# First conditioning weights, norm and first V, q, k products taken in two halves of the features; rope tables on two engines

## The chip, the cores and the metric

The kernel runs on one core of a Trainium2 chip. The metric is the device time of one execution in microseconds (us), shown as the median of several runs. One further execution was recorded by the hardware profiler; every row below comes from it. Engines are named as the profile names them: PE is TensorE (PEld its weight loads), DVE is VectorE, ACT is ScalarE, POOL is GpSimd, SP is the queue that issues the DMAs.

## The reference

Two transformer blocks over 512 tokens of 1024 features. Only the opening of the first block is touched by the change:

```python
def first_block(x, c, positions, ada_w, ada_b, norm_mix_g, ...):
    cond = jax.nn.silu(c)
    for layer in range(DEPTH):
        mod = (cond @ ada_w[layer] + ada_b[layer])[:, None, :]
        shift_m, scale_m, gate_m, shift_f, scale_f, gate_f = jnp.split(mod, 6, axis=-1)
        h = rmsnorm(x, norm_mix_g[layer]) * (1.0 + scale_m) + shift_m
        ...
            mixed = attention_head_groups(h, positions, attn_w_in[i], attn_w_out[i])
```

`attention_head_groups` multiplies `h` by `attn_w_in` to get q, k and V; q and k of the first group of heads are turned by `partial_rope` with the cosine and sine of position times frequency.

## The kernel before

Everything is in float32, feature by token: `x` is eight tiles of 128 features x 512 tokens (k = 0..7). To keep precision each factor of a product is split into a high and a low part (`hh`, `hl` of `h`; `whi`, `wlo` of the weights), and `mm3` (L243, L244, L245) adds three products for each k. The order of the instructions on each engine is set before the run by a scheduler that lists them by data and program order; each engine then works through its own list in that order and stops where an operand is missing.

The opening of `block1` does this. The queue SP loads constants, `x`, the positions (`pi`) and then 32 tiles `araw` of the conditioning weights, 128x512 each, twelve buffers deep. Each `araw` is multiplied by the vector `cond`: for half of the four column groups on PE (L306, one output row), for the others on DVE (L309 and L311, into `acc`). L328 turns each sum of 512 into four columns of `mod` (four matmuls with a vector of ones), and L330 adds the bias. Groups 2 and 3 of 512 columns make the scale (all of A, L336, before the shift's weights come), groups 0 and 1 the shift B. Beside it `mean_squares` (L377, L378, L383), `rstd` (on POOL, `rs_r`) and `bcast_rows` (L367, into PSUM) make the reciprocal root of the norm. `modulated` then makes `t2u` = x A r (L396, DVE), `hh` = `t2u` + B (L397, ACT) and `hl` (L398, DVE), and only with that can the first products start: V of the first four heads (96 matmuls of 256 columns), then q and k of the first two heads (24 matmuls of 512 columns each).

After it, `project` turns q and k by the rope tables (L669 to L673), splits them and copies them by DMA into `stk`, `stk2h` and `stk2l` (L684), the operands of the first scores `sc` (L729). The products q and k of the next two heads are in PE's list between the first k and the first scores, and so fill PE while the rope chain runs.

`rope_tables` makes both tables on POOL, one after the other with the same scratch tiles. Its instructions stand in POOL's list before and after `rs_r`.

Of the kernel before, what the change touches and what calls it, by code (L numbers as in the profile page):

```python
# [9 lines left out]
F32 = mybir.dt.float32  # L10
# [129 lines left out]
class Net:  # L140
# [95 lines left out]
            steps.append(step)  # L236
        return steps

    def mm3(self, out, terms):

        n = len(terms)
        for j, (lh, ll, rh, rl) in enumerate(terms):
            self.nc.tensor.matmul(out, lhsT=lh, rhs=rh, start=j == 0, stop=False)  # L243
            self.nc.tensor.matmul(out, lhsT=ll, rhs=rh, start=False, stop=False)  # L244
            self.nc.tensor.matmul(out, lhsT=lh, rhs=rl, start=False, stop=j == n - 1)  # L245

    def mm_fm(self, out, w, c0, h, kt=KD, m=P):

# [342 lines left out]
        if cols:  # L591
            nc.vector.tensor_mul(dst, u, ps[0:64, n:2 * n])

    def v_heads(self, pool, w, c0, h, n, tag, bufs=1):


        V = pool.tile([P, n // P, 4, 2, 64], F32R, tag=tag, bufs=bufs, name="V")
        for t in range(0, n // P, 2):
            ps = self.psum()
            for i in range(2):  # L600
                self.mm_tm(ps[:, i * 256:i * 256 + 256], w, c0, 256, h, t + i)
            src = ps.rearrange("p (t h d) -> p t h d", t=2, h=4)
            self.split(V[:, t:t + 2, :, 0], V[:, t:t + 2, :, 1], src)
        return V

    def rope_tables(self, pool, work):

        nc = self.nc
        eng = nc.gpsimd
        pi = work.tile([P, T], I32, name="pi")  # L610
        nc.sync.dma_start(pi, self.a["pos"].to_broadcast([P, T]))
        ang, k, t, r = [work.tile([P, T], F32, name="rp_" + n) for n in ("ang", "k", "t", "r")]
        eng.tensor_copy(ang, pi)
        eng.tensor_scalar(ang, ang, self.c_inv, None, op0=ALU.mult)

        c1 = 6.28125
        c2 = math.floor((TWO_PI - c1) * 2 ** 20) / 2.0 ** 20
        c3 = TWO_PI - c1 - c2
        magic = 1.5 * 2.0 ** 23
        lim = 3.1415925  # L620
        out = []
        for name, turn in (("cos", 0.25), ("sin", 0.0)):
            eng.tensor_scalar(k, ang, 1.0 / TWO_PI, turn, op0=ALU.mult, op1=ALU.add)
            eng.tensor_scalar(k, k, magic, None, op0=ALU.add)
            eng.tensor_scalar(k, k, magic, None, op0=ALU.subtract)
            for c, y in ((c1, ang), (c2, r), (c3, r)):
                eng.tensor_scalar(t, k, c, None, op0=ALU.mult)
                eng.tensor_sub(r, y, t)
            if turn:
                eng.tensor_scalar(r, r, math.pi / 2, None, op0=ALU.add)  # L630
            o = pool.tile([P, T], F32, name="rp_" + name)
            eng.tensor_scalar(o, r, lim, -lim, op0=ALU.min, op1=ALU.max)
            out.append(o)

        def finish():
            for o in out:
                self.tc.keep_in_program_order(nc.scalar.activation(o, o, AF.Sin))
            eng.tensor_scalar(out[1], out[1], self.c_sgn, None, op0=ALU.mult)
            return out
        return finish  # L640

    def attention(self, x, h, gate, w_in, w_out, norms):
        nc = self.nc
        swap = [(j + 8 if j < 8 else j - 8) if j < 16 else j for j in range(32)]
        with self.pool("early", side="right") as ep, self.pool("att") as ap:
            self.work = self.letters(ep, b=2) | self.letters(ap, d=2) | dict(big=(ap, "stk1", 2))
            self.exp_and_ln(h[1][:, KD - 1])
            cos, sin = self.rope_cs
# [4 lines left out]
            def project(c, m, V):  # L653

                part, base = c // 2, c // 2 * 1536
                c0 = base + c % 2 * 256
                if m == 0:
                    w = self.wchunk(w_in[:, c0 + 1024:c0 + 1280], "k")
                    V = self.v_heads(ap, w, 0, h, T, "V", 2)
                    self.w_qk = [self.wchunk(w_in[:, c0 + j * 512:c0 + j * 512 + 256]) for j in range(2)]  # L660
                st = []
                for j in range(2):
                    ps = self.psum()
                    self.mm_fm(ps, self.w_qk[j], m * P, h)
                    scale = 0.125 if j == 0 else 1.0
                    hl = [ap.tile([P, T], F32R, tag="s" + x, bufs=2, name="s" + x) for x in "hl"]
                    if part == 0:
# [1149 lines left out]
    def block1(self, x):  # L1817
# [7 lines left out]
        b = self.v("ada_b", 0, 48)  # L1825
        with self.pool("rope", side="right") as rp:
            with self.dense():
                for k in range(0, KD, 4):
                    nc.sync.dma_start(x[:, k:k + 4], a["xT"][k * P:(k + 4) * P].rearrange("(k p) t -> p k t", p=P))
                self.c_inv = self.load_const(rp, "inv")  # L1830
                self.c_sgn = self.load_const(rp, "sgn")
                with self.pool("acc", side="right") as self.accp:
                    rope = self.rope_tables(rp, self.accp)
                    self.causal = self.load_const(rp, "causal", BF16)
                    self.lt01 = self.load_const(rp, "lt01")
                    self.ltneg = self.load_const(rp, "ltneg", BF16)
                    self.negtri = self.load_const(rp, "negtri", F32R)
                    self.work["u"] = (self.accp, 8, "t2u", T)
                    tasks = self.ada_tasks(a["ada_w"][0], (1, 0), [cond], [mod], b, 12, "dn", (1, 3), False)
                    A = fx.tile([P, KD], F32, tag="A1", bufs=3, name="A")  # L1840
                    h, ((stats, apply),) = self.hnorm(x, T, A, mod[:, 0:8], size=T)
                    w = a["attn_w_in"][0][:, 1024:1280]
                    loads = self.load_ahead(*[(w, 0, k, "k") for k in (0, 4)])
                    for i in range(32):
                        tasks[i // 16 * 16 + (1 - i % 2) * 8 + i % 16 // 2]()
                        if i == 7:
                            stats()
                        if i == 15:
                            self.gain_scale(A, self.v("norm_mix_g", 0, 8), mod, 1)
                    for load in loads:  # L1850
                        load()
                    apply()
# [11 lines left out]
            self.attention(x, h, mod[:, 16:24], a["attn_w_in"][0], a["attn_w_out"][0],  # L1864
                           lambda: norms("norm_ffn_g", 0, 3, *self.ffn_first(*self.gate_up(a["ffn_w_in"][0]))))
# [69 lines left out]
```

## Time and profile before

| what | value |
| --- | --- |
| median of 3 runs | 3423.15 us (3422.83 to 3424.58) |
| profiled execution, its time | 3421.65 us |
| its span | 3419.9 us |
| mean granted clock of PE, of full speed | 0.981 |
| PE busy | 3247.7 us (95%) |
| DVE busy | 2228.5 us (65%) |
| ACT busy | 1275.0 us (37%) |
| POOL busy | 100.0 us (3%) |

The span is the recorded part of the execution; the profiled execution took 1.75 us more than its span and 1.5 us less than the median of the runs. Busy is the share of the span in which an engine had an instruction in work. All times in the rows count from the start of the span.

### The profile page before, as it was taken

To read this page: it belongs to the slowest core of one execution; us is meant where nothing else is said; L and a number is where in the kernel's file an instruction comes from. 1 tells how busy PE (TensorE), PEld (TensorE's weight loads), DVE (VectorE), ACT (ScalarE), POOL (GpSimd) and SP (SyncE) were. 2 spreads that over 40 slices of the span, in tenths; PEclk is the share of its full clock that TensorE was granted. 3 is DMA by queue.
4 is the path that set the end of the run, shared out by engine and by line. 5 is a ranking of instruction groups with operands and counts; after the bars stand their busy time and mean duration, and the time that the engine had idled before them with its cause. 6 is when DMAs were issued, how large, how long until landed. Compare 5 with 4: busy or idle time off the path is not lost.

```text
span 3419.9 us, 46640 instructions
## 1 busy us (share of the span) xinstructions
PE 3247.7 (95%) x17648; PEld 2666.4 (78%) x17648; DVE 2228.5 (65%) x4569; ACT 1275.0 (37%) x2467; POOL 100.0 (3%) x142
## 2 busy tenths in 40 slices
PE   7998999999999899998999989999999889889999
PEld 4886788878778787887777768888887776778886
DVE  6977655568988677677878777534445875753334
ACT  3566422235443332223644443212123455542222
POOL 4000000001000000000000000000000000000000
PEclk9999999999999999999999999999999999999999
DMA  6645355532111254553343323333332443413332
GB/s 226 173 134 163 119 168 157 158 114 62 44 50 56 64 172 138 163 167 108 115 133 89 113 62 98 113 95 111 117 111 75 114 133 102 127 50 96 96 97 76
DMA packets 480081, 389.76 MB, mean 114 GB/s; under 512 B 21360, under 2 KB 390128, under 8 KB 479856
## 3 DMA queue, kind: packets, MB, share of 16 engines
q1 hardware_dynamic: 479856, 386.77, 37.9%
q8 instruction: 139, 2.28, 0.3%
q14 instruction: 86, 0.70, 0.1%
HBM read 356.28 MB, written 17.83 MB: 109 GB/s over the span
## 4 chain that ended last, share of the span: by engine, by line
PE 43%; DVE 4%; ACT 3%; issue 1%; DMA 1%; POOL 0%; POOLq 0%; DVEq 0%; ACTq 0%
PE dn L243 6%; PE dn L244 6%; PE dn L245 6%; PE d L243 6%; PE d L245 6%; PE d L244 6%; PE s L1244 1%; PE tp L1208 1%; PE tp L1227 1%; PE tp L1234 1%; DVE cv L1373 1%; ACT pr L1187 1%; DVE wlo L173 1%; PE dn L378 1%; DVE st L1184 0%
## 5 line engine op out<-in xcount | busy, mean ns | idle before, releaser
L172 ACT CAST whi<-raw 128x1024 fp32r<-128x1024 f32 (+1 forms) x399 | 417.1, 1046 | 782.7 <-PE d L245 411.3
L173 DVE TENSOR_TENSOR wlo<-raw,whi 128x1024 fp32r<-128x1024 f32 (+1 forms) x399 | 486.3, 1220 | 268.5 <-ACT whi L172 267.8
L243 PE MATMUL dn<-hh,whi 128*128 128x512 f32 (+1 forms) x1688 | 619.7, 368 | 8.9 <-ACT t2b L1358 4.5
L245 PE MATMUL dn<-hl,whi 128*128 128x512 f32 (+1 forms) x1688 | 614.0, 365 | 0.0
L244 PE MATMUL dn<-hh,wlo 128*128 128x512 f32 (+1 forms) x1688 | 613.3, 364 | 0.0
L243 PE MATMUL d<-hh,whi 128*128 128x512 f32 (+1 forms) x1120 | 400.7, 358 | 0.0
L244 PE MATMUL d<-hh,wlo 128*128 128x512 f32 (+1 forms) x1120 | 399.9, 357 | 0.0
L245 PE MATMUL d<-hl,whi 128*128 128x512 f32 (+1 forms) x1120 | 399.8, 357 | 0.0
L243 PEld LDWEIGHTS dn<-hh,whi 128*128 128x128 f32 x1688 | 321.4, 191 | 57.8 <-ACT t2b L1358 5.2
L245 PEld LDWEIGHTS dn<-hl,whi 128*128 128x128 f32 x1688 | 321.1, 191 | 46.5 <-issue 2.7
L244 PEld LDWEIGHTS dn<-hh,wlo 128*128 128x128 f32 x1688 | 321.7, 191 | 42.7 <-issue 1.4
L311 DVE SCALAR_TENSOR_TENSOR acc<-araw,cond,acc 128x512 f32<-128x512 f32 x322 | 241.9, 751 | 68.3 <-DMA araw<-in_ada_w 38.7
L243 PE MATMUL d<-gh,whi 128*128 128x512 f32 (+1 forms) x696 | 252.3, 363 | 0.4 <-ACT gh L172 0.4
L244 PE MATMUL d<-gh,wlo 128*128 128x512 f32 (+1 forms) x696 | 249.8, 359 | 0.0
L245 PE MATMUL d<-gl,whi 128*128 128x512 f32 (+1 forms) x696 | 248.6, 359 | 0.0
L243 PEld LDWEIGHTS d<-hh,whi 128*128 128x128 f32 x1120 | 210.7, 188 | 32.6 <-issue 1.3
L244 PEld LDWEIGHTS d<-hh,wlo 128*128 128x128 f32 x1120 | 210.7, 188 | 32.5 <-issue 1.3
L245 PEld LDWEIGHTS d<-hl,whi 128*128 128x128 f32 x1120 | 210.7, 188 | 31.6 <-DVE hl L398 0.9
L243 PEld LDWEIGHTS d<-gh,whi 128*128 128x128 f32 x696 | 130.6, 188 | 27.9 <-issue 3.5
L245 PEld LDWEIGHTS d<-gl,whi 128*128 128x128 f32 x696 | 130.1, 188 | 24.5 <-issue 2.2
L244 PEld LDWEIGHTS d<-gh,wlo 128*128 128x128 f32 x696 | 130.6, 188 | 23.5 <-issue 2.2
L515 DVE TENSOR_TENSOR t2b<-t2a,d 128x512 f32<-128x512 f32 (+1 forms) x67 | 42.0, 627 | 150.7 <-PE d L245 150.7
(507 smaller groups left out, 5641.9 us busy)
## 6 DMA issues: line engine op xcount, KB each, us to landing
araw<-in_ada_w SPq DMA_DIRECT2D x192, 256.0 KB, 3.7
araw<-in_w_ada SPq DMA_DIRECT2D x192, 256.0 KB, 3.0
raw<-in_ffn_w_in SPq DMA_DIRECT2D x88, 512.0 KB, 4.2
raw<-in_ffn_w_out SPq DMA_DIRECT2D x44, 512.0 KB, 4.4
raw<-in_w_in SPq DMA_DIRECT2D x44, 512.0 KB, 3.8
raw<-in_w_gate SPq DMA_DIRECT2D x44, 512.0 KB, 3.9
raw<-in_w_up SPq DMA_DIRECT2D x44, 512.0 KB, 3.8
raw<-in_w_down SPq DMA_DIRECT2D x44, 512.0 KB, 3.6
```

The costliest lines, as they stand in the source:

```text
L172: nc.scalar.copy(hi, src)
L173: nc.vector.tensor_sub(lo, src, hi.bitcast(F32))
L243: self.nc.tensor.matmul(out, lhsT=lh, rhs=rh, start=j == 0, stop=False)
L244: self.nc.tensor.matmul(out, lhsT=ll, rhs=rh, start=False, stop=False)
L245: self.nc.tensor.matmul(out, lhsT=lh, rhs=rl, start=False, stop=j == n - 1)
L311: nc.vector.scalar_tensor_tensor(st[i], raw, s, st[i], op0=ALU.mult, op1=ALU.add)
L378: nc.tensor.matmul(sums, lhsT=weights(k), rhs=sq, start=k == 0, stop=k == KD - 1)
L515: nc.vector.tensor_mul(y, s, pu[:, :n])
L1187: nc.scalar.activation(pr, s, AF.Exp, bias=st[:, 0:1], accum_out=st[:, 2:3])
L1208: nc.tensor.transpose(tp[:, n * P:(n + 1) * P], pr[:, c:c + P], self.ident)
L1227: nc.tensor.matmul(ps[:64, q0:q1], lhsT=lhs, rhs=pt[sl // 2][0][:, sl % 2, q0:q1].bitcast(F32), start=j == 0, stop=j == nb - 1, skip_group ...
L1234: nc.tensor.matmul(ps[:, q0:q1], lhsT=lhs, rhs=pt[sl // 2][i][:, sl % 2, q0:q1], start=j == 0 and i == 0, stop=j == nb - 1 and i == 1, ski ...
```

## The change

The 32 tasks of the conditioning weights are taken in another order: first the tiles of scale and shift for features 0 to 511, then those for features 512 to 1023. After each half A and B of these features are known, `hh` and `hl` of its four k are made, and the products of V, q and k are added up over these four k only. Four PSUM banks (two `tp` for q and k, two `dn` for V) hold the sums from the first half to the second. The norm is no longer folded into `t2u`: `xr` = x r is made once for all eight k on DVE as soon as the broadcast r stands in PSUM; then `hh` = A xr + B on ACT and `t2u`, `hl` on DVE. The conditioning work on PE is now the shift (groups 0 and 1), that on DVE the scale. The first weights of V, q and k are loaded between the conditioning weights.

The sine table moves from POOL to DVE, with scratch tiles of its own, and the first two steps of the angle too; the positions are loaded before `x` and no longer after it.

```diff
+    def mm3(self, out, terms, start=True, stop=True, **kw):
...
-        eng = nc.gpsimd
...
-        eng.tensor_copy(ang, pi)
-        eng.tensor_scalar(ang, ang, self.c_inv, None, op0=ALU.mult)
+        nc.vector.tensor_copy(ang, pi)
+        nc.vector.tensor_scalar(ang, ang, self.c_inv, None, op0=ALU.mult)
...
-        for name, turn in (("cos", 0.25), ("sin", 0.0)):
+        for name, turn, eng in (("cos", 0.25, nc.gpsimd), ("sin", 0.0, nc.vector)):
+            k, t, r = [work.tile([P, T], F32, name="rp_" + n + name) for n in "ktr"]
...
+    def opening(self, x, A, B, w_in):
...
+        ws = self.wchunk(w_in[:, 1024:1280], "k"), self.wchunk(w_in[:, :256]), self.wchunk(w_in[:, 512:768])
+        v, qk = [], []
+
+        def norm():
+            r = self.rstd(self.mean_squares(self.norm_work(), x, self.mean_col)[:, :, 0], 4)
+            rb = self.bcast_rows(r, 4)
+            for k in range(KD):
+                nc.vector.tensor_mul(xr[:, k], x[:, k], rb)
+
+        def part(k0):
+            ks = range(k0, k0 + 4)
+            for k in ks:
+                nc.scalar.activation(hh[:, k], xr[:, k], AF.Identity, bias=B[:, k:k + 1], scale=A[:, k:k + 1])
+                u = self.t2("u")
+                nc.vector.tensor_scalar(u, xr[:, k], A[:, k:k + 1], B[:, k:k + 1], op0=ALU.mult, op1=ALU.add)
+                nc.vector.tensor_sub(hl[:, k], u, hh[:, k].bitcast(F32))
...
+            how = dict(start=k0 == 0, stop=k0 > 0)
+            for out, w in zip(qk, ws[1:]):
+                self.mm3(out, [(*w(k, 0, P), hh[:, k], hl[:, k]) for k in ks], **how)
+            for t in range(4):
+                s = slice(t * P, t * P + P)
+
+                self.mm3(v[t // 2][:, t % 2 * 256:t % 2 * 256 + 256],
+                         [(hh[:, k, s], hl[:, k, s], *ws[0](k, 0, 256)) for k in ks],
+                         start=k0 == t % 2 == 0, stop=k0 > 0, skip_group_check=True)
...
-                for k in range(0, KD, 4):
-                    nc.sync.dma_start(x[:, k:k + 4], a["xT"][k * P:(k + 4) * P].rearrange("(k p) t -> p k t", p=P))
...
                     rope = self.rope_tables(rp, self.accp)
+                    for k in range(0, KD, 4):
+                        nc.sync.dma_start(x[:, k:k + 4], a["xT"][k * P:(k + 4) * P].rearrange("(k p) t -> p k t", p=P))
...
-                    tasks = self.ada_tasks(a["ada_w"][0], (1, 0), [cond], [mod], b, 12, "dn", (1, 3), False)
+                    tasks = self.ada_tasks(a["ada_w"][0], (1, 0), [cond], [mod], b, 12, "d2", (2, 3), False)
...
-                    for i in range(32):
-                        tasks[i // 16 * 16 + (1 - i % 2) * 8 + i % 16 // 2]()
-                        if i == 7:
-                            stats()
...
+                    for half in range(2):
+                        for i in range(16):
+                            tasks[i % 2 * 16 + half * 8 + i // 2]()
+                            if (half, i) == (0, 3):
+                                norm()
+                            if (half, i) == (1, 3):
+                                loads.pop(0)()
+                        c = half * 4
...
+                        for _ in range((2, 1)[half]):
+                            loads.pop(0)()
+                        part(c)
```

What this does to the lists of the engines is seen at three places. In the names, `d_...` and `dn` are PSUM sums of the conditioning weights or of V, `tp` is the PSUM bank of the norm and, in the changed kernel, of q and k.

First, PE's list of before from the broadcast of r (L367) to the first product:

```order
L367 MATMUL tp<-c_ident,rs_r 128x128 x4
L306 MATMUL dn<-araw,cond 1x512 x3
L328 MATMUL dn<-one,row 128x1 x4
L328 MATMUL d_252<-one,acc 128x1 x4
L306 MATMUL d_261<-araw,cond 1x512 x8
L328 MATMUL d_308<-one,row 128x1 x4
```

The same place in the changed kernel, to the first product of q over k = 0:

```order
L367 MATMUL tp<-c_ident,rs_r 128x128 x4
L306 MATMUL d_168<-araw,cond 1x512 x4
L328 MATMUL d_258<-one,acc 128x1 x4
L328 MATMUL d_269<-one,row 128x1 x4
L306 MATMUL d_392<-araw,cond 1x512 x2
L243 MATMUL tp<-hh,whi 128x512
```

And further down in it, from the last product of V over the first half to the first products of q and k over the second:

```order
L245 MATMUL dn<-wlo,hh 128x256
L306 MATMUL d_392<-araw,cond 1x512 x5
L328 MATMUL d_433<-one,acc 128x1 x4
L306 MATMUL d_392<-araw,cond 1x512
L328 MATMUL d_444<-one,row 128x1 x4
L243 MATMUL tp<-hh,whi 128x512
```

So 24 matmuls of 512 and 48 of 256 columns moved up between the second and the third conditioning tile of the second half; six such tiles and two turnings of `mod` now stand behind them.

Second, PE's list around the first scores, before (L729 is `sc`):

```order
L243 MATMUL dn<-hh,whi 128x512
L244 MATMUL dn<-hh,wlo 128x512
L245 MATMUL dn<-hl,whi 128x512
L729 MATMUL sc<-stk2h,stk_538 128x256 x2
L243 MATMUL dn<-hh,whi 128x512
```

and in the changed kernel (L777 is `sc`):

```order
L243 MATMUL dn<-hh,whi 128x512
L244 MATMUL dn<-hh,wlo 128x512
L777 MATMUL sc<-stk2h,stk_582 128x256 x2
L245 MATMUL dn<-hl,whi 128x512
L243 MATMUL dn<-hh,whi 128x512
```

Between the end of V, q and k of the first heads and these scores stand 36 products of the next heads before, and 12 now. From some 190 us of the span on, the lists of the two kernels are the same on all engines.

Third, DVE's list from its first conditioning tile on, before:

```order
L309 TENSOR_SCALAR acc<-araw,cond 128x512
L311 SCALAR_TENSOR_TENSOR acc<-araw,cond,acc 128x512 x3
L356 TENSOR_SCALAR rs_v<-tp 128x4
L311 SCALAR_TENSOR_TENSOR acc<-araw,cond,acc 128x512 x4
L330 TENSOR_TENSOR mod<-dn,vec 128x4
```

and in the changed kernel, from the last step of the sine table on (eleven instructions of the tables stand ahead of it):

```order
L635 TENSOR_SCALAR rp_sin<-rp_rsin 128x512
L309 TENSOR_SCALAR acc<-araw,cond 128x512
L311 SCALAR_TENSOR_TENSOR acc<-araw,cond,acc 128x512 x4
L356 TENSOR_SCALAR rs_v<-tp 128x4
L311 SCALAR_TENSOR_TENSOR acc<-araw,cond,acc 128x512
L659 TENSOR_TENSOR xr<-x,tp 128x512 x8
L311 SCALAR_TENSOR_TENSOR acc<-araw,cond,acc 128x512
L173 TENSOR_TENSOR wlo<-raw,whi 128x1024
L311 SCALAR_TENSOR_TENSOR acc<-araw,cond,acc 128x512
L173 TENSOR_TENSOR wlo<-raw,whi 128x1024
L330 TENSOR_TENSOR mod<-d_258,vec 128x4
```

The eight `xr` and one split of weights now stand ahead of the last sums on which the first half of A waits.

## Rows read from the trace of the kernel before

**Rows 1.** The page: busy time, share of the span and instructions of each engine.
```profile
PE 3247.7 (95%) x17648; PEld 2666.4 (78%) x17648; DVE 2228.5 (65%) x4569; ACT 1275.0 (37%) x2467; POOL 100.0 (3%) x142
```
**Rows 2.** Windows: stretch, length, busy PE, PEld, DVE, ACT, POOL, clock, DMA share, GB/s.
```profile
20.00:30.00 10.00, 8.47 (x39) 3.98 (x39) 4.24 (x9) 0.58 (x1) 7.98 (x6) 1.00 1.05 389
...
40.00:50.00 10.00, 4.31 (x16) 3.64 (x16) 8.04 (x11) 6.97 (x11) 9.49 (x7) 0.50 0.20 55
```
**Rows 3.** Timeline of DVE: start, us, line, operation, count, idle before it.
```profile
39.99 2.54 DVE L311 SCALAR_TENSOR_TENSOR acc<-araw,cond,acc 128x512 f32<-128x512 f32 x3
```
**Rows 4.** Timeline of PE, from the last conditioning sum to the first scores.
```profile
42.58 1.87 PE L328 MATMUL d<-one,acc 128*128 128x1 f32 x8 [4.26 <-DVE acc L311]
45.46 0.79 PE L243 MATMUL dn<-whi,hh 128*128 128x256 f32 x2 [1.01 <-ACT hh L397]
...
58.08 0.28 PE L243 MATMUL dn<-whi,hh 128*128 128x256 f32 x1
58.20 0.28 PE L244 MATMUL dn<-whi,hl 128*128 128x256 f32 x1
...
63.96 0.40 PE L243 MATMUL dn<-hh,whi 128*128 128x512 f32 x1
...
74.64 0.39 PE L245 MATMUL dn<-hl,whi 128*128 128x512 f32 x1
...
84.76 0.40 PE L729 MATMUL sc<-stk2h,stk 128*128 128x256 f32 x2
```
**Rows 5.** Windows of half a microsecond in which the granted clock changes (columns as Rows 2).
```profile
38.50:39.00 0.50, 0.00 (x0) 0.00 (x0) 0.50 (x2) 0.00 (x0) 0.50 (x1) 0.70 1.07 375
...
55.50:56.00 0.50, 0.50 (x5) 0.50 (x5) 0.50 (x2) 0.50 (x1) 0.00 (x0) 0.74 0.00 0
```
**Rows 6.** Timeline of PE at full clock: conditioning tiles (two records each) and a turning.
```profile
23.80 2.73 PE L306 MATMUL dn<-araw,cond 128*1 128x512 f32 x6
...
37.28 1.05 PE L328 MATMUL d<-one,row 1*128 1x1 f32 x8 [0.72 <-ACT row L317]
```
**Rows 7.** Timeline of POOL: the root of the norm, and steps of the rope tables.
```profile
21.68 1.48 POOL L360 TENSOR_TENSOR rs_r<-rs_v,mhalf 128x4 f32<-128x4 f32 x1 [4.14 <-DVE rs_v L356]
...
30.65 1.58 POOL L627 TENSOR_SCALAR rp_t<-rp_k 128x512 f32<-128x512 f32 x1
32.31 1.26 POOL L628 TENSOR_TENSOR rp_r<-rp_r,rp_t 128x512 f32<-128x512 f32 x1
...
34.68 1.49 POOL L630 TENSOR_SCALAR rp_r<-rp_r 128x512 f32<-128x512 f32 x1
...
40.19 1.90 POOL L627 TENSOR_SCALAR rp_t<-rp_k 128x512 f32<-128x512 f32 x1
```
**Rows 8.** Timeline of DVE beside them.
```profile
31.28 0.48 DVE L309 TENSOR_SCALAR acc<-araw,cond 128x512 f32<-128x512 f32 x1
...
32.34 1.78 DVE L311 SCALAR_TENSOR_TENSOR acc<-araw,cond,acc 128x512 f32<-128x512 f32 x1
...
35.36 0.74 DVE L311 SCALAR_TENSOR_TENSOR acc<-araw,cond,acc 128x512 f32<-128x512 f32 x1
```
**Rows 9.** Timeline of DVE in the rope chain, and a split of weights.
```profile
71.12 0.69 DVE L671 TENSOR_TENSOR t2b<-t2b,rp_sin 128x512 f32<-128x512 f32 x1
71.72 0.68 DVE L672 TENSOR_TENSOR t2a<-t2a,rp_cos 128x512 f32<-128x512 f32 x1
...
75.41 1.22 DVE L173 TENSOR_TENSOR wlo<-raw,whi 128x1024 fp32r<-128x1024 f32 x1
```
**Rows 10.** Timelines of ACT (split of k) and of SP (its copies to the operand).
```profile
80.25 0.62 ACT L172 CAST sh<-t2a 128x512 fp32r<-128x512 f32 x1 [3.33 <-DVE t2a L673]
...
80.89 1.10 SPq L684 DMA_DIRECT2D stk2h<-sh  x2
```
**Rows 11.** DMA issues of the first 130 us: count, KB each, median us to landing.
```profile
stk2h<-sh SPq DMA_DIRECT2D x8, 128.0 KB, 2.4
...
pi<-in_pos SPq DMA_DIRECT2D x1, 256.0 KB, 7.9
```

More of the change, by code (lines that the diff above doesn't have):

```diff
@@ L592, in merge_heads, with v_heads @@
             nc.vector.tensor_mul(dst, u, ps[0:64, n:2 * n])
-    def v_heads(self, pool, w, c0, h, n, tag, bufs=1):
+    def v_heads(self, pool, w, c0, h, n, tag, bufs=1, made=None):
         V = pool.tile([P, n // P, 4, 2, 64], F32R, tag=tag, bufs=bufs, name="V")
         for t in range(0, n // P, 2):
-            ps = self.psum()
-            for i in range(2):
-                self.mm_tm(ps[:, i * 256:i * 256 + 256], w, c0, 256, h, t + i)
+            if made:
+                ps = made.pop(0)
+            else:
+                ps = self.psum()
+                for i in range(2):
+                    self.mm_tm(ps[:, i * 256:i * 256 + 256], w, c0, 256, h, t + i)
             src = ps.rearrange("p (t h d) -> p t h d", t=2, h=4)
@@ L608, in rope_tables @@
         nc = self.nc
-        eng = nc.gpsimd
         pi = work.tile([P, T], I32, name="pi")
         nc.sync.dma_start(pi, self.a["pos"].to_broadcast([P, T]))
-        ang, k, t, r = [work.tile([P, T], F32, name="rp_" + n) for n in ("ang", "k", "t", "r")]
-        eng.tensor_copy(ang, pi)
-        eng.tensor_scalar(ang, ang, self.c_inv, None, op0=ALU.mult)
+        ang = work.tile([P, T], F32, name="rp_ang")
+        nc.vector.tensor_copy(ang, pi)
+        nc.vector.tensor_scalar(ang, ang, self.c_inv, None, op0=ALU.mult)
         c1 = 6.28125
@@ L637, in finish, with attention @@
                 self.tc.keep_in_program_order(nc.scalar.activation(o, o, AF.Sin))
-            eng.tensor_scalar(out[1], out[1], self.c_sgn, None, op0=ALU.mult)
+            nc.vector.tensor_scalar(out[1], out[1], self.c_sgn, None, op0=ALU.mult)
             return out
         return finish
-    def attention(self, x, h, gate, w_in, w_out, norms):
+    def opening(self, x, A, B, w_in):
+        nc = self.nc
+        h = self.h_parts(T)
+        hh, hl = h
+        xr = self.accp.tile([P, KD, T], F32, name="xr")
+        ws = self.wchunk(w_in[:, 1024:1280], "k"), self.wchunk(w_in[:, :256]), self.wchunk(w_in[:, 512:768])
[12 more added lines that the diff above has]
+                nc.vector.tensor_sub(hl[:, k], u, hh[:, k].bitcast(F32))
+            if not v:
+                v.extend(self.pa.tile([P, 512], F32, tag="dn", bufs=2, name="dn") for _ in range(2))
+                qk.extend(self.pa.tile([P, 512], F32, tag="tp", bufs=2, name="tp") for _ in range(2))
+            how = dict(start=k0 == 0, stop=k0 > 0)
[6 more added lines that the diff above has]
+                         start=k0 == t % 2 == 0, stop=k0 > 0, skip_group_check=True)
+        return h, ws, norm, part, (v, qk, ws[1:])
+    def attention(self, x, h, gate, w_in, w_out, norms, opened):
         nc = self.nc
@@ L656, in project @@
                 c0 = base + c % 2 * 256
-                if m == 0:
+                first = c == m == 0
+                if first:
+                    V = self.v_heads(ap, None, 0, h, T, "V", 2, opened[0])
+                    self.w_qk = opened[2]
+                elif m == 0:
                     w = self.wchunk(w_in[:, c0 + 1024:c0 + 1280], "k")
@@ L662, in project @@
                 for j in range(2):
-                    ps = self.psum()
-                    self.mm_fm(ps, self.w_qk[j], m * P, h)
+                    if first:
+                        ps = opened[1][j]
+                    else:
+                        ps = self.psum()
+                        self.mm_fm(ps, self.w_qk[j], m * P, h)
                     scale = 0.125 if j == 0 else 1.0
```

26 lines of the change are left out of this document (12 added, 14 removed).

## The prediction

> **What bounds the kernel now.** The page first: PE is busy 95% of the span, the next engine 65% [rows 1]. A change can pay only where PE waits or runs slowly, and the opening is such a place. The windows show it: from 20 to 30 us PE is busy 8.47 of 10 us at full clock, from 40 to 50 us only 4.31, at a granted clock of 0.50 [rows 2]. DVE's timeline says why: the sums over the conditioning weights end at 42.53 (39.99 + 2.54) [rows 3]. PE's timeline follows on: it turns the last sum at 42.58, starts the first product at 45.46, the first q at 63.96, the last of k at 74.64, and reaches the first scores at 84.76 [rows 4]. The windows of half a microsecond give the clock: it falls from 2.4 to 1.2 GHz in 38.5 to 39.0, after PE had little to do, and rises again in 55.5 to 56.0 [rows 5].
>
> **The yardstick.** Later work has the same order in both kernels, and PE is full there, so I compare the two at the first scores. Before, 36 products of the next heads are done by then; after, 12. A product of 512 columns takes (74.64 - 63.96) / 47 = 0.227 us [rows 4], so the changed kernel owes 24 x 0.227 = 5.5 us more work there. It breaks even if its scores start at 84.76 - 5.5 = 79.3 us.
>
> **The change, step by step**, on the clock of the span.
>
> 1. *r in PSUM.* Before, `rs_r` runs on POOL at 21.68, as soon as DVE has its input [rows 7]; with its 1.48 us and four transposes r stands at 23.9, since PE goes on to its next tile at 23.80 [rows 6]. Now it stands behind the whole cosine table in POOL's list. `pi` took 7.9 us to land behind `x`; ahead of it I give it what other small loads take, 2.4 us [rows 11], so about 5.3 us; DVE's cast and scaling take 2 x 0.48 [rows 8], POOL starts at 6.4. Its list to `rs_r` is six one-input steps of about 1.5, three two-input steps of 1.26 [rows 7], three casts, a short first step and a short last one, which I put at 2.5 together, and 14 gaps of 0.1: 16.7 us, to 23.1. With `rs_r` and the transposes r stands at 25.3. Contention adds: a POOL step that met a DVE instruction took 1.90, not 1.49 [rows 7]; DVE makes the sine meanwhile. I take 25.5. Ends: 23.9 (as now) and 32 (the lock, below).
>
> 2. *First half of A.* DVE's list from there to the last sum: eight `xr` at 0.60 (71.12 to 71.72), a sum of 0.7, a split of 1.22 and a sum of 0.75 [rows 8, 9]: 7.4 us, to 32.9. The loads hide here: conditioning tiles were at DVE before that and wait in their buffers.
>
> 3. *Turning, and two tiles.* PE has had nothing since its fourth tile behind r (25.5 + 4 x 0.9 = 29), as before 38.5, when the clock fell. So I price at 1.2 GHz: two turnings of 1.87 [rows 4], to 36.6, and the two tiles that stand ahead of the first product. A tile is 2.73 / 3 = 0.9 at full clock (steps of 0.86) [rows 6], 1.7 at half: 3.4, to 40.0. At full clock it would be 2 x 1.05 + 1.7, to 36.7; that is the low end. `hh`, `t2u` and `hl` of four k take DVE 4 x (0.4 + 0.6) and run beside it.
>
> 4. *First half of the products.* 24 x 0.227 + 48 x 0.12 (58.08 to 58.20 [rows 4]) = 11.2 us at full clock. The tiles of step 3 are dense work, so I let the clock return 2 us into it, which costs 1 us: 52.2. The rest of the weights is loaded meanwhile. The third weight tile must wait until DVE has split the first (about 32), and twelve conditioning tiles stand behind it; at 0.68 us each, the 262 KB of one at the 389 GB/s of the stretch from 20 to 30 us [rows 2], they land by 45. Nothing waits for them, since PE is in its products.
>
> 5. *The second half's conditioning* stands on PE behind these: five tiles (4.3), a turning (1.0), a tile (0.9), `row` on ACT (0.6), a turning (1.0), the bias and the first `hh` (0.9), hand-overs (0.3): 9.0 us, to 61.2. Here is what the change gives back: before, the same tiles ran on PE beside the loads, when it had nothing else to do.
>
> 6. *Second half of the products.* q and k: 5.5, to 66.7. In step 5 PE has some 4 us of small work, as it had ahead of 38.5 [rows 5], so I let the clock fall once more and charge 1.5 us: k ends at 68.2. V 5.8 and the 12 products 2.7: PE is at the scores at 76.7.
>
> 7. *The rope chain.* From the end of k (75.03) to the scores it took 9.7 us, and PE filled it with 36 products. Now q and k end together and DVE must turn both: from the first shuffle, 0.7 us ahead of k's end, thirteen instructions at about 0.65 (two `acc`, two halves of V's split among them) bring k's sum at 7.7 us, the split of ACT 0.62, two issues 1.1 [rows 10], landing 2.4 [rows 11]: 11.5 us behind k's end with hand-overs, so 79.7. PE waits 3 us there.
>
> So 79.7 against 79.3: the changed kernel loses 0.4 us. Against the profiled execution's 3421.65 that is 3422.05; the median of the runs shown lies 1.5 us higher, so I predict **3423.5 us**: no change that a measurement could tell. What can be told is 0.2%, 6.8 us. PE starts its products 5 us earlier and loses less to the clock, but has 9 us of conditioning between them and a chain that has lost its cover.
>
> **A rule weighed.** A one-input DVE step of 0.48 us (31.28) ran while POOL was in a one-input step (30.65 + 1.58), at its usual length; a sum with two inputs (35.36) took its 0.74 beside a one-input POOL step (34.68 + 1.49). But a sum at 32.34 took 1.78: it began just behind a two-input POOL step (32.31 + 1.26) and ended some 0.5 us after it [rows 7, 8]. So two-input steps of POOL hold DVE up and one-input steps hardly do. The Trainium skill, page "SBUF — State Buffer", section "SBUF: two separate sides", goes further: DVE instructions in a two-port mode, or with two inputs in SBUF, and those of POOL exclude each other, and the second waits for the whole first. By the page the two table chains would take turns; the trace agrees for the two-input step alone. What turns would cost is the second rival.
>
> **The rivals.** *(a) The clock stays up and the chain is no longer than now.* For it: PE's work up to 29 us is dense, and q can be turned while k runs. r at 23.9, step 2 to 31.3, step 3 at full clock to 35.1, step 4 to 46.3, step 5 to 55.3, k to 60.8, the scores 9.7 later: 70.5, 8.8 us ahead of the yardstick: 3414.3 us. Against it: PE stands idle for about 4 us in step 3 and once more in step 5, and the fall at 38.5 came after less. One of the two alone (the clock up throughout, the chain as in step 7) gives about 74, 3418, which is no change by the bound.
>
> *(b) POOL and DVE take turns.* Ten steps of the sine (5.4 us of DVE) alternate with POOL's: POOL ends its table at 23.1 + 5.4 = 28.5, and DVE, which waits for a POOL step of 1.5 each time, ends the sine at 6.4 + 10 x 2.0 = 26.4, then has five sums (3.1) ahead of `rs_v`: 29.7. r stands at 32, 6.5 later than I took, and all behind it moves: +6.9, 3430 us. It decides from r at 31.9 on: that is where the loss passes 6.8 us. For it the 1.78; against it the two unhindered steps at 31.28 and 35.36.
>
> *(c) The first half gains nothing*, since the extra weights ahead of the second half delay its sums. PE asks for those tiles only at 52 and they land by 45; seven us late would be needed. It adds little to the spread.
>
> **How the numbers follow.** My forecast (within 0.2%) gets 0.62; (a) and its like 0.24; (b) 0.10 and other losses, such as a chain held by DVE's late `acc` tiles, 0.04. That makes 0.24 faster, 0.62 same, 0.14 slower. The forecast's own range is 3417 to 3429, from 3 us of clock to either side and the ends of step 7. With (a) and most of (b), 8 in 10 lies between 3413 and 3430.
>
> **What would show it.** `rs_r` on POOL ends at about 24.5 (31 by (b)); the clock of PE is 0.50 at 34 and back by 43; the first product of q starts near 40, L306 comes back near 52, the first product of the second half near 61, and PE stands 3 us before the scores at about 79.7. I am wrong if the scores start before 72.5 or after 86, or if the work behind them does not keep the distance.

## The result, and the profile after

The changed kernel takes 3442.76 us (median of 4 runs, 3439.28 to 3446.93), the kernel before 3422.99 us beside it: a ratio of 1.0058, 95% interval 1.0046 to 1.0071. It is 19.8 us slower; "no change" was forecast, and the time lies outside the range. The span of the profiled execution is 3441.8 us, 21.9 us longer.

First PE's timeline of the changed kernel in the opening, which answers to [rows 4, 6]:

```profile
26.61 1.12 PE L367 MATMUL tp<-c_ident,rs_r 128*128 128x128 f32 x4 [2.04 <-POOL rs_r L360]
27.65 6.14 PE L306 MATMUL d<-araw,cond 128*1 128x512 f32 x8
37.33 1.87 PE L328 MATMUL d<-one,acc 128*128 128x1 f32 x8 [3.53 <-DVE acc L311]
39.13 1.86 PE L328 MATMUL d<-one,row 1*128 1x1 f32 x8
40.91 3.57 PE L306 MATMUL d<-araw,cond 128*1 128x512 f32 x4
44.42 0.80 PE L243 MATMUL tp<-hh,whi 128*128 128x512 f32 x1
...
65.99 0.50 PE L243 MATMUL tp<-hh,whi 128*128 128x512 f32 x1 [1.10 <-ACT hh L664]
...
80.48 0.50 PE L243 MATMUL dn<-hh,whi 128*128 128x512 f32 x1 [1.17 <-DVE V L173]
...
82.88 0.51 PE L244 MATMUL dn<-hh,wlo 128*128 128x512 f32 x1 [1.90 <-DVE wlo L173]
...
86.37 0.63 PE L777 MATMUL sc<-stk2h,stk 128*128 128x256 f32 x2
```

The first q starts at 44.42, the second half at 65.99, the scores at 86.37. Before, they started at 84.76 [rows 4], so they come 1.6 us later, with 24 fewer products done by then. By the yardstick of the prediction (break-even at 79.3) that is 7.1 us lost ahead of the scores. The rest of the 22, some 15 us, is lost later, where the forecast did not look. The windows of the changed kernel (columns as in [rows 2]) show the place:

```profile
100.00:110.00 10.00, 6.96 (x47) 5.76 (x45) 8.74 (x22) 4.91 (x14) 0.00 (x0) 1.00 0.34 97
110.00:120.00 10.00, 3.70 (x17) 3.71 (x18) 9.62 (x15) 0.83 (x2) 0.00 (x0) 0.57 0.74 220
```

PE is busy 3.70 us of 10, at a clock of 0.57, while DVE is busy 9.62. PE's timeline there:

```profile
107.02 0.40 PE L587 MATMUL pv<-c_ident,smx 128*128 128x128 f32 x2
116.30 0.58 PE L245 MATMUL dn<-wlo,hh 128*128 128x256 f32 x1 [8.87 <-DVE wlo L173]
```

It waits 8.87 us for `wlo`, the low part of the weights for the next V. The high part had been made by ACT long before, as ACT's timeline shows:

```profile
95.25 1.06 ACT L172 CAST whi<-raw 128x1024 fp32r<-128x1024 f32 x1
98.00 1.06 ACT L172 CAST whi<-raw 128x1024 fp32r<-128x1024 f32 x1
```

DVE's timeline says why the low part is late. It takes its instructions in the order of its list, and these stand ahead of the split, which starts with no idle time before it:

```profile
109.55 0.75 DVE L311 SCALAR_TENSOR_TENSOR acc<-araw,cond,acc 128x512 f32<-128x512 f32 x1
110.22 0.68 DVE L173 TENSOR_TENSOR sl<-t2a,sh 128x512 fp32r<-128x512 f32 x1
111.05 0.75 DVE L311 SCALAR_TENSOR_TENSOR acc<-araw,cond,acc 128x512 f32<-128x512 f32 x1
...
112.93 0.68 DVE L719 TENSOR_TENSOR t2b<-t2b,rp_sin 128x512 f32<-128x512 f32 x1
113.75 0.75 DVE L311 SCALAR_TENSOR_TENSOR acc<-araw,cond,acc 128x512 f32<-128x512 f32 x1
114.42 0.68 DVE L720 TENSOR_TENSOR t2a<-t2a,rp_cos 128x512 f32<-128x512 f32 x1
115.02 1.22 DVE L173 TENSOR_TENSOR wlo<-raw,whi 128x1024 fp32r<-128x1024 f32 x1
```

Between 96.3, where the first cast is done, and 115.02 eight background sums (`acc`, one of 0.48 and seven of some 0.74 us, 5.7 in all) and seven steps of the next heads' rope chain (4.8 us) run on DVE, with softmax work of the heads between them. In the kernel before, the last split ahead of V's first product (90.17) ran at 85.11, as DVE's timeline shows, and between the scores and 195 us PE waited for no split:

```profile
85.11 1.22 DVE L173 TENSOR_TENSOR wlo<-raw,whi 128x1024 fp32r<-128x1024 f32 x1
```

**The account.** Both kernels meet again in one instruction: the first `sl` of the second group of heads, from which PE and DVE have the same work in the same order. It starts at 195.69 before and at 218.96 after, 23.3 us later. Up to there I count, from 10 us on, what PE lost: idle is the length of a stretch less PE's busy time (rows of windows below: before, then after, ahead of the scores and behind them; only PE is shown); the clock's loss is busy time times the missing share of the granted clock, summed over windows of at most 1 us.

```profile
10.00:84.76 74.76, 62.99 (x280) 0.89 0.69 223
84.76:195.69 110.93, 108.35 (x689) 1.00 0.54 149
```

```profile
10.00:86.37 76.37, 65.58 (x248) 0.85 0.60 193
86.37:218.96 132.59, 119.47 (x721) 0.94 0.50 141
```

| kernel | idle ahead of scores | clock ahead | idle behind | clock behind | sum | common point |
| --- | --- | --- | --- | --- | --- | --- |
| before | 11.8 | 4.4 | 2.6 | 0.0 | 18.8 | 195.69 |
| after | 10.8 | 10.5 | 13.1 | 4.8 | 39.2 | 218.96 |

So 15.3 of the 20.4 us that PE loses more lie behind the scores. Ahead of them the changed kernel idles 1.0 us less, as it should, and loses 6.1 us more to the clock. The 2.9 us between 20.4 and 23.3 this count doesn't find. All these figures, and those of the stages below, are from one profiled execution of each kernel. Behind the common point the profiled executions of all runs took between 3221.1 and 3229.8 us, so a few microseconds won or lost ahead of it are told by the medians alone.

### The profile page after: what moved, and what is told of

Same layout as the page of the kernel before. It is cut to its first block, busy times and chain, and to the rows that moved or that the text cites. A ratio compares the mean times of both kernels' runs of the same rounds, so it can differ in the third digit from the quotient of the medians.

```text
span 3441.8 us, 46649 instructions
## 1 busy us (share of the span) xinstructions
PE 3259.4 (95%) x17648; PEld 2671.9 (78%) x17648; DVE 2237.2 (65%) x4591; ACT 1275.2 (37%) x2467; POOL 81.4 (2%) x129
## 4 chain that ended last, share of the span: by engine, by line
PE 42%; DVE 5%; ACT 3%; issue 1%; DMA 1%; POOL 0%; POOLq 0%; SPq 0%; DVEq 0%; ACTq 0%
PE dn L243 6%; PE dn L244 6%; PE dn L245 6%; PE d L243 6%; PE d L245 6%; PE d L244 6%; PE s L1292 1%; PE tp L1256 1%; PE tp L1275 1%; PE tp L1282 1%; DVE cv L1421 1%; DVE wlo L173 1%; ACT pr L1235 1%; DVE st L1232 1%; PE dn L378 1%
## 5 line engine op out<-in xcount | busy, mean ns | idle before, releaser
L243 PEld LDWEIGHTS d<-hh,whi 128*128 128x128 f32 x1120 | 210.7, 188 | 32.6 <-issue 1.3
L244 PEld LDWEIGHTS d<-hh,wlo 128*128 128x128 f32 x1120 | 210.7, 188 | 32.5 <-issue 1.3
L243 PEld LDWEIGHTS d<-gh,whi 128*128 128x128 f32 x696 | 130.6, 188 | 27.7 <-issue 3.5
```

The source lines that it names most:

```text
L243: self.nc.tensor.matmul(out, lhsT=lh, rhs=rh, start=start and j == 0, stop=False, **kw)
```

## The experiments

Theory A: most of the loss is the late split in DVE's list, and the half clock that follows. Theory B: DVE is simply the bound there, and would make PE wait for something else. Theory C: the opening makes all of the loss. All ratios are to the kernel before, on the same chip.

**e1: fewer background sums in the first pair of heads.**

```diff
-TICKS = (11, 0, 0, 0, 10, 10, 10, 10)
+TICKS = (5, 6, 0, 0, 10, 10, 10, 10)
```

> The changed kernel with 8 of the 16 background sums of the first pair of heads moved to the second pair (first pair asks for 5 x 1.5 steps, the second for 6 x 1.5); nothing is left out. Theory A (late split): most of the loss behind the first scores is PE's wait of 8.9 us at 107 to 116 for a weight split (wlo) of the next V that stands in DVE's list behind background sums and the rope chain, and the half clock that follows (2.7 us). Some six sums of 0.66 us fewer stand ahead of it, so the split comes about 4 us earlier and the time falls by 4 to 6 us, to about 3438. Theory B (DVE is the bound there: its list is 96% full from 110 to 120, so the same work ends when it ends): the sums taken out shorten the stage, but come back in the second pair, where DVE is over 90% busy too: 3441 to 3444. Theory C (all of the loss is made ahead of the first scores): no change, 3443.

3436.98 us, ratio 1.0041 (1.0028 to 1.0054): 5.8 us less than the 3442.76, within the 4 to 6 us of theory A. PE's timeline shows the one wait become two shorter ones, the first for the background sums themselves:

```profile
108.56 1.62 PE L328 MATMUL st<-one,acc 128*128 128x1 f32 x8 [3.79 <-DVE acc L311]
...
111.97 0.58 PE L245 MATMUL dn<-wlo,hh 128*128 128x256 f32 x1 [1.79 <-DVE wlo L173]
```

**e2: the next V's weights ahead of the background sums.**

```diff
-                        self.tick(TICKS[i])
+                        if i:
+                            self.tick(TICKS[i])
                         if i < 7:
                             V, st = project(*pairs[i + 1], V)
+                        if i == 0:
+                            for load in self.load_ahead(*[(w_in[:, 1280:1536], 0, k, "k") for k in (0, 4)]):
+                                load()
+                            self.tick(TICKS[i])
```

> The changed kernel, in which the two loads and splits of the next V's weights are asked for right behind the second pair's q and k, and the background sums of the first pair behind them; the same instructions in another order, nothing is left out. Theory A (late split): the first split now stands in DVE's list ahead of the first softmax, the second in the middle of the pair's heads; PE has V's products as cover and does not stand at 107 to 116. The wait of 8.9 us and the half clock behind it (116 to 122, 2.7 us) go: about 3431. Theory B (DVE is the bound in that stage, PE's wait only shows it): the sums pushed back come later in the same stage and PE waits for another DVE instruction in its place: 3440 to 3443. Theory C (the loss is made ahead of the first scores): 3443.

3422.94 us, ratio 1.0001 (0.9993 to 1.0010). All that the change lost is back, with the same instructions in another order; B and C fall. A fell short too: it foresaw 3431. The edit did more than bring the late split forward: ahead of the scores the list changed as well, and 24 products of the next heads stand there in place of 12. Two rows show the rest: the splits of DVE, the first now ahead of the first softmax, and PE's windows ahead of the scores and behind them.

```profile
83.47 1.23 DVE L173 TENSOR_TENSOR wlo<-raw,whi 128x1024 fp32r<-128x1024 f32 x1 [0.95 <-ACT whi L172]
93.08 1.21 DVE L173 TENSOR_TENSOR wlo<-raw,whi 128x1024 fp32r<-128x1024 f32 x1
```

```profile
10.00:83.54 73.54, 64.63 (x260) 0.88 0.61 201
83.54:198.56 115.02, 111.71 (x709) 1.00 0.59 163
```

Behind the scores PE idles 3.3 us in place of 13.1, and nothing is lost to the clock. Ahead of them the waits of 1.17 and 1.90 us are down to one of 0.63, and the scores start at 83.54. The common point comes at 198.56, 20.4 us earlier than in the changed kernel and still 2.9 later than before.

**e11: the same two splits on POOL.**

```diff
...
-                self.split(hi, lo, raw)
+                if src.tensor.name == "in_attn_w_in" and n == 256 and cut == "k" and src.offset == 1280:
+                    nc.scalar.copy(hi, raw)
+                    nc.gpsimd.tensor_sub(lo, raw, hi.bitcast(F32))
+                else:
+                    self.split(hi, lo, raw)
```

> The changed kernel, in which the two wlo splits of the next V's weights run on POOL in place of DVE; loads, sums and q, k come in the changed kernel's order up to the first scores; nothing is left out. POOL is idle there, a two-input step of 512 took it 1.27 us, so the two take about 2.5 us each behind the casts at 95 and 98 and are done by 102. Theory A (the split's place in DVE's list is the cause): PE's wait of 8.9 us at 107 to 116 and the half clock behind it are gone, 11 to 15 us less, 3428 to 3432. Theory B (DVE is full there, PE would wait for its softmax, V or rope chain instead): at most the 2.4 us that DVE is spared, 3440 or more.

3429.90 us, ratio 1.0022 (1.0013 to 1.0030), 12.9 us less than the changed kernel and inside theory A's 3428 to 3432. The opening is the changed kernel's, in the same order on PE, DVE and ACT up to the scores (q at 44.14, scores at 86.19). POOL's timeline shows the splits end by 101.3, and in the list of PE's waits between the scores and the common point (205.53) the longest is 0.9 us:

```profile
96.08 2.40 POOL L222 TENSOR_TENSOR wlo<-raw,whi 128x1024 fp32r<-128x1024 f32 x1 [69.68 <-ACT whi L221]
98.83 2.44 POOL L222 TENSOR_TENSOR wlo<-raw,whi 128x1024 fp32r<-128x1024 f32 x1 [0.34 <-PE sc L783]
```

```profile
PE tp L789 <- ACT pr L809: 0.9, 2, 0.7
PE pv L799 <- DVE t2d L596: 0.9, 1, 0.9
```

DVE was spared 2.4 us and PE gained 13: that is the split's place, not DVE's load. What is left, 8.0 us above the 3421.91 of the kernel before beside it, is what the opening loses; it agrees with the 7.1 us of the yardstick.

**e3: the rope tables on POOL again, `x` loaded first** (`rope_tables` and the place of the loads as before; halves kept).

```diff
...
-        for name, turn, eng in (("cos", 0.25, nc.gpsimd), ("sin", 0.0, nc.vector)):
+        for name, turn in (("cos", 0.25), ("sin", 0.0)):
...
```

> The changed kernel with the rope tables as before (both on POOL, x loaded ahead of the positions); the halves of the features stay; nothing is left out. DVE's list from the splits on is that of the changed kernel. If the tables on two engines cost the opening time (r stood at 26.6 us where it stood at 23.2, and DVE's conditioning sums were behind the sine): r is back at about 23.5, the last sum of the first half ends near 33, the first product of q starts near 41 (44.4 in the changed kernel), the scores near 83, and the time falls by about 3 us to 3440. If the conditioning's loads set the first half (rival): q starts at 44 as in the changed kernel and the time stays at 3443. The wait at 107 to 116 stays in both cases, since nothing behind the scores is moved.

3440.68 us, ratio 1.0053 (1.0040 to 1.0066). q starts at 36.72, 7.7 us earlier and more than expected, but the scores at 83.10, only 3.3 earlier. The wait stays, as PE's timeline shows:

```profile
113.43 0.58 PE L245 MATMUL dn<-wlo,hh 128*128 128x256 f32 x1 [9.10 <-DVE wlo L173]
```

The common point comes 3.5 us earlier (215.44). By these starts the tables cost the opening some 3 us, no more; the difference of the medians, 2.1 us, is within the intervals.

**e4: e2 and e3 together.**

> The two edits of the runs before together: tables on POOL as before, and the next V's weights ahead of the background sums. If the two losses are independent the gains add: 3443 - 3 - 11.7 = about 3428, still 5 us above the kernel before, which is what the opening itself would then lose. If DVE bounds the stage behind the scores: 3440.

3421.65 us, ratio 0.9999 (0.9991 to 1.0008). That is 6 us under the 3428 that were foreseen from e2's expected gain, and no more than e2 alone reached: the gains do not add. The scores start at 83.07, the common point is at 199.47.

**e7 and e8: the kernel before with one part alone**, its tables made on two engines as in the changed kernel (e7), or its V weights taken early as in e2 (e8).

> The kernel before with one part of the change alone: the rope tables made on POOL and DVE, the positions loaded ahead of x; nothing is left out. By the changed kernel's trace the sine slows DVE's conditioning sums (its one-input steps took 0.71 to 0.86 us beside POOL) and r comes 3 us later, while before the conditioning ends only at 42.5 by its loads. If the loads set it: no change, 3423 (3420 to 3426). If DVE's lateness passes on to the last sum (rival): 3 us late or more, 3426 to 3430. A late split behind the scores, as in the changed kernel, could come by a new order too: 3435 or more would show that.

> The kernel before with the early loads and splits of the next V's weights and the background sums behind them; nothing is left out. Its PE did not wait for a split behind the scores, so if the edit mends only what the change broke, the time stays at 3423 (3420 to 3426). If the edit is a gain of its own, which hid a real loss of the changed kernel (rival), the time falls below 3419.

e7: 3423.62 us, ratio 1.0004 (0.9995 to 1.0013). r's transposes come at 28.18 and the first product some 3 us later than before (48.59), but waits of 1.92 and 1.59 us between V's products shrink to 0.55 us and less, and q starts at 63.89, where it did. e8: 3420.66 us, ratio 0.9994 (0.9985 to 1.0003). Neither can be told from the kernel before: without the halves the tables cost nothing that these runs can tell, and e2's edit is a repair, not a gain of its own.

**e5 and e6: the second half's conditioning inside the first half's products**, on e4 and on e2. V's products become a function `vpart`, called behind the second half's tiles:

```diff
...
+                        if half:
+                            vpart(0)
                         part(c)
+                    vpart(4)
```

> The run with both edits (tables on POOL, early V weights), in which the program also asks for the second half's conditioning tiles ahead of the first half's V products, so that on PE five tiles and both turnings stand between products of q, k and V; the same work, nothing is left out. In the run before it PE stood 0.66 + 1.10 us at 60 to 62.5 between two turnings, and its clock was 0.66 over 60 to 70. If this gap is what the opening still loses (theory A), the second half's products start near 57 in place of 62.5, the clock stays at full speed, and the scores start 4 to 5 us earlier: about 3417. If the rope chain or DVE holds the scores (rival): the second half starts earlier, but the scores still start near 82 and the time stays at 3421.

> The same edit on the changed kernel with early V weights (tables still made on two engines); nothing is left out. There the second half's products started at 64.2 and PE stood 0.66 + 1.10 us ahead of them. Theory A: they start near 59, the time falls by 4 to 5 us to about 3418. Rival (rope chain or DVE holds the scores): 3422 to 3423.

3421.69 us (1.0002, 0.9994 to 1.0011) and 3422.50 us (1.0000, 0.9991 to 1.0009). In both PE's waits of 0.66 and 1.10 us are gone. The second half's products do not start earlier, which was not expected (62.25 against 62.47 in e4, 64.86 against 64.21 in e2), since the first half's V now stands ahead of them; but q and k then run without the half clock, and V begins at 67.72 in e5 against 70.94 in e4. In both PE now stands right ahead of the scores, which start at 81.39 and 83.70, for the copies to `stk2h` (1.62 and 0.85 us). The times are the rival's: the rope chain holds the scores.

**e9, e10 and e12: PE kept busy ahead of the first half's turning**, on e5, e2 and e6, by four products that nobody reads (from 27.9 us on in e9, 32.6 in e10, 33.5 in e12):

```diff
                 nc.vector.tensor_mul(xr[:, k], x[:, k], rb)
+            keep = self.psum("d2")
+            for _ in range(4):
+                nc.tensor.matmul(keep[:1], lhsT=self.mean_d[:, :1], rhs=xr[:, KD - 1], start=True, stop=True)
```

> The run with the conditioning tiles inside the products (tables on POOL, early V weights), with four products more on PE whose result nobody reads (one row of 512 from the last xr each); nothing is left out. In that run PE had nothing from 27.4 to 32.2, its clock was 0.50 from 32 to 42, and this cost 4.7 us. If the clock falls because PE has nothing to do there: the clock stays at full speed, the two turnings take 1.05 us in place of 1.87, q starts near 35.5 in place of 37.6, and the scores start 3 to 5 us earlier: 3417 to 3418 where the run without them gives 3421.7. If DVE's list sets the first products and the rope chain the scores (rival): the clock rises, but the scores start near 81 as before and the time stays at 3421 to 3422.

> The same four products in the changed kernel with early V weights (tables on two engines); nothing is left out. There the clock cost 7.8 us ahead of the scores, in two falls: from 30 to 46 and from 62 to 67. The first is covered here, the second is not. If the clock is what the opening loses: 4 to 5 us less before the scores, about 3418.5. If the second half's conditioning and the rope chain give it back (rival): 3422 to 3423.

> The changed kernel with early V weights, the second half's conditioning tiles inside the first half's products, and the four products that keep PE busy (tables on two engines); nothing is left out. Both gaps of the opening are covered here. If what the opening saves reaches the end when the order behind the scores lets it: the first products of q near 40, the second half's near 55, the scores near 78, and 3 to 4 us less than the kernel before, 3418 to 3419. If the list that is planned behind the scores gives it back, as in the run with tables on POOL (rival): 3421 to 3427.

| run | us | ratio (interval) | q | scores | idle, clock ahead | idle, clock behind | common point |
| --- | --- | --- | --- | --- | --- | --- | --- |
| e2 | 3422.94 | 1.0001 (0.9993 to 1.0010) | 42.73 | 83.54 | 8.9, 7.8 | 3.3, 0.0 | 198.56 |
| e10 | 3423.12 | 1.0004 (0.9995 to 1.0013) | 39.93 | 79.64 | 5.3, 2.8 | 5.0, 0.0 | 196.27 |
| e9 | 3426.66 | 1.0012 (1.0003 to 1.0021) | 35.92 | 81.78 | 6.9, 3.4 | 4.8, 2.9 | 199.40 |
| e12 | 3416.94 | 0.9989 (0.9980 to 0.9998) | 42.35 | 79.77 | 2.5, 4.8 | 1.8, 0.0 | 192.02 |

(The columns are those of the account above; q and scores are starts on PE; the four products, 3.6 us, count as busy.) The windows from 30 to 40 us show the clock of e2, then of e10 and of e12:

```profile
30.00:40.00 10.00, 6.47 (x21) 0.67 0.38 125
```

```profile
30.00:40.00 10.00, 9.42 (x34) 1.00 0.40 123
```

```profile
30.00:40.00 10.00, 9.90 (x32) 0.84 0.24 72
```

In e10 the clock stays up, and the scores start 3.9 us earlier; 2.3 of these are left at the common point, and the median is the rival's 3423. In e12 the same four products stand in the same order up to the first q, and yet the clock was 0.50 until 32.5 and fell again at 39, while PE was at work. So work in the gap does not settle the clock by itself; what does, these runs don't tell. e9 met neither expectation (3417 to 3418, or 3421 to 3422): it is slower than the kernel before, by less than the 0.2% that I called telling. Behind its scores the list came out differently once more, and PE's timeline has a wait for the copies, where e5's PE stood 1.11 us; no run shows that this wait is what makes it slower:

```profile
146.96 0.76 PE L788 MATMUL sc<-stk2h,stk 128*128 128x256 f32 x2 [3.26 <-DMA stk2h<-sh]
```

In e12, where both gaps of the opening are covered and no such wait follows, the common point is 3.7 us ahead of the kernel before, and the median 3.9 us lower. Its interval lies below 1, but by less than those 0.2%. The way was not the one foreseen: q starts at 42.35, not near 40, and the second half at 62.16, not near 55.

## Why the prediction was wrong

**The step that failed** is the yardstick: "Later work has the same order in both kernels, and PE is full there, so I compare the two at the first scores." It put all that lies behind the scores at nothing, although the section on the change says that the lists are the same only from some 190 us on. Between the scores and the common point the changed kernel's lists differ, and with them the split's place on DVE: PE stood 8.87 us and lost the clock, 15.3 us of the account. e11, which takes away that and little else, gives 12.9 us back.

**A second step failed too**, the sum that puts the scores at 79.7, 0.4 us behind break-even. They came at 86.37, so 7.1 us behind it, and e11, which keeps this opening, is still 8.0 us above the kernel before. Had the yardstick held, these 6.7 us alone would have brought the forecast of 3423.5 to some 3430, outside its range as well. e2's 3422.94 does not speak for the sum: it has the stretch ahead of the scores mended too.

**Point by point.**

1. *r in PSUM*: forecast 25.5, its transposes ran at 26.61 + 1.12, so 27.7. POOL's list took what was worked out, 18.5 us from its first step at 8.08 to the end of `rs_r` (16.7 + 1.48 foretold); it began 1.7 us late, since `pi` landed at 7.0, not 5.3: it took 4.4 us from its issue, not the 2.4 that I had read off the copies to `stk2h`, which are half its size.
2. *Last sum*: forecast 32.9, it ended at 37.3. Beside the 2.2 us of step 1, DVE stood 2.09 us for a `whi`, whose cast stood on ACT behind the copy of `row`, which waited for PE's four tiles (27.65 + 6.14). Those I had at 4 x 0.9 us, at full clock; but the granted clock had fallen to 0.50 (1.2 GHz) in PE's wait of 2.04 us for `rs_r`, and rose again only at 32.5. I had priced DVE's list and not this wait. In e1, whose opening has the same order, the clock rose by 30.5, the tiles took 4.55 us and DVE stood 0.49. The rows stand behind this list.
3. *Turning and two tiles*: q at 44.42, forecast 40.0; the length, 7.1 us, is as priced (32.9 to 40.0), at half clock throughout.
4. and 5. *First half and second conditioning*: PE was through the first half at 56.79 and began the second at 65.99, so 12.4 and 9.2 us; forecast 12.2 and 9.0. Right.
6. and 7. *Second half and chain*: the scores came 20.4 us behind its start, forecast 18.5 (61.2 to 79.7). PE waited there for V's split and the next weights (1.17 and 1.90), with the clock falling twice more, and not for the chain's copies: no wait stands ahead of the scores. The chain's own sum had a slip besides: its terms add up to 11.8 us, not 11.5.

To point 2, the changed kernel first: a window of PE (only PE is shown), then the timelines of ACT and of DVE; and the timelines of PE and of DVE in e1:

```profile
26.50:32.50 6.00, 5.89 (x10) 0.50 0.48 170
```

```profile
33.84 0.57 ACT L317 COPY row<-d 1x512 f32<-1x512 f32 x1 [11.45 <-PE d L306]
34.32 1.99 ACT L172 CAST whi<-raw 128x1024 fp32r<-128x1024 f32 x2
```

```profile
35.39 1.23 DVE L173 TENSOR_TENSOR wlo<-raw,whi 128x1024 fp32r<-128x1024 f32 x1 [2.09 <-ACT whi L172]
```

```profile
28.40 4.55 PE L306 MATMUL d<-araw,cond 128*1 128x512 f32 x8
```

```profile
34.54 1.23 DVE L173 TENSOR_TENSOR wlo<-raw,whi 128x1024 fp32r<-128x1024 f32 x1 [0.49 <-ACT whi L172]
```

"PE starts its products 5 us earlier and loses less to the clock": the first product came 1.0 us earlier (44.42 against 45.46), and the clock took 10.5 us against 4.4. Two of the forecast's own signs of being wrong were met: the scores start after 86, and the work behind them does not keep the distance (110.93 us to the common point before, 132.59 after).

**The rivals.** (a) did not come: the clock fell, and from k's end to the scores it took 13.0 us in place of 9.7; e10, on e2, shows the clock up from 30 to 60 us, and that the median does not show it. (b) did not come either: r stood at 27.7, not 32, and e7 finds the tables alone free. (c) did not come: PE's tiles at 56.79 ran without a wait. The true case, 19.8 us, was in none of them: I had looked for a way to be slower in the opening only.

**The rule weighed** said that one-input steps of POOL hardly hold DVE up. The changed kernel's timelines of POOL and DVE say otherwise:

```profile
9.01 1.55 POOL L627 TENSOR_SCALAR rp_kcos<-rp_kcos 128x512 f32<-128x512 f32 x1
...
13.89 1.32 POOL L631 TENSOR_TENSOR rp_rcos<-rp_ang,rp_tcos 128x512 f32<-128x512 f32 x1
```

```profile
9.24 0.71 DVE L628 TENSOR_SCALAR rp_ksin<-rp_ksin 128x512 f32<-128x512 f32 x1
...
14.12 1.63 DVE L631 TENSOR_TENSOR rp_rsin<-rp_rsin,rp_tsin 128x512 f32<-128x512 f32 x1
```

A DVE step inside a one-input step of POOL took 0.71 us and ended before POOL's did (9.95 against 10.56); the scaling of the angle at 7.50, with POOL idle, took 0.49. The sum of [rows 8] at 31.28, a step of one input too, kept its 0.48; what tells the two apart no run here separates. A step of DVE with two inputs, begun inside a two-input step of POOL, took 1.63 and ended 0.5 us after it; one begun at 10.87 inside a one-input step of POOL (10.64 + 1.54) took 0.97 and ended inside it. The Trainium skill, page "SBUF — State Buffer", section "SBUF: two separate sides", has the second of two instructions that exclude each other wait for the whole first; the trace agrees for two inputs beside two inputs, and shows slower steps but no full wait beside a one-input step of POOL.

**What stays open**: why the list that is planned puts the split so late. That its place is the cause of some 13 of the 19.8 us is shown; the planner's reason is not. The edits moved other instructions too, since each makes the lists anew. Of the opening's 7 to 8 us the places are shown, but not what each costs at the end, nor what makes the clock fall at one time and not at another.

## What to carry to other kernels

A point at which two kernels are compared stands for the end only if what lies behind it is compared too: where lists are planned anew, read on each engine that feeds the bound one what now stands ahead of the next operand that it will ask for. A wait of the bound engine behind a full in-order list can be mended by moving a few instructions: 13 us here for two splits put on an engine that stood idle. An earlier start is not yet time won: 7.7 us at the first product were 4.1 at the second half and 3.3 at the scores in e3, and 3.9 at the scores became 2.3 at the common point in e10. And one experiment that brings the whole time back does not show one cause: e2 mended two losses at once, and only e11, which keeps the opening, tells them apart.

## What the runs showed of the hardware that I had not expected

Less idle time did not mean less lost to the clock: the changed kernel idled 1.0 us less than the one before ahead of the scores, and lost 6.1 us more to 1.2 GHz (10.5 against 4.4). The clock fell at 26, in PE's wait of 2.04 us, and at 36, in one of 3.53.

The same order does not give the same clock each time: up to the first q the changed kernel, e1, e2 and e11 have the same lists on PE, DVE and ACT, and the four tiles behind r took 6.14, 4.55, 5.29 and 6.03 us in them. Four products without a reader, 3.6 us of PE, went with a clock of 2.4 GHz from 30 to 40 us in e10 (1.00 in place of 0.67), and in e12 with 0.84.
